# Seven block products in place of eight, for the attention groups' and the output projections of a hybrid attention/retention block

## The chip, the cores and the metric

One core of one Trainium2 chip runs the whole kernel. The metric is the device time of one execution in microseconds (us), as the median of the runs shown. All data come from and go back to the chip's own memory (HBM).

## The reference, cut to what matters

One layer on 4096 tokens of width 1024. `x` is normalised by RMS, then one input projection gives the parts of eight attention heads (width 64: q, k, v, a gate z, and a forget logit f for each head) and of four retention heads (width 128: q, k, v, gate z). The heads' outputs are gated, joined to 1024 columns, and go through an output projection, a second RMS norm and the residual sum.

```python
u    = rms_norm(h, pre_norm_gain)
proj = einsum('bsd,de->bse', u, w_in)            # 1024 -> 4104 columns
fq, fk, fv, fz, ff, rq, rk, rv, rz = split(proj)
c    = cumsum(log_sigmoid(ff + bias))
fox  = softmax(fq.fk/8 + c[t] - c[s], causal) @ fv * silu(fz)
ret  = group_norm(chunkwise_retention(rotary(rq), rotary(rk), rv)) * silu(rz)
out  = einsum('bse,ed->bsd', concat(fox, ret), w_out)
h    = h + rms_norm(out, post_norm_gain)
```

Everything is wanted in near-float32 accuracy, so each operand of a projection is held as two float16 parts, `hi` and `lo = x - hi`, and a product takes three matmul passes: hi.hi, hi.lo and lo.hi (`PASSES`).

## The kernel before, in words

**Work and groups.** Tokens are handled in 8 blocks of 512 (`NB`). The projections are cut into five groups: 0 and 1 (attention heads 0 to 3 and 4 to 7), 2 and 3 (retention heads), and 4 (output). Each input group has two parts of 512 columns: part 0 (q and k) gives its result transposed (`unit_T`: the weight is the stationary operand, 512 token columns move), part 1 (v and z) gives it token by token (`unit_N`: the tokens are stationary, 512 weight columns move; in group 0 the forget logits make it 520, run as 256 and 264). One unit is 8 steps over the 1024 inputs (`KT`) times 3 passes. A block of one part is four units, so 96 matmuls of 512 columns.

**Stages.** `phase_f0` runs group 0 over all blocks. Beside it the next block of x is loaded, normalised (`a_norm`), transposed on TensorE against the identity and split into hi and lo (`a_k`, L349 to L355), and stored to HBM as `XT`, from where the later groups load it again (`xt_load`). Then `attention` runs over 64 items (head, query block). Each of its 1152 steps makes one tile of scores (two matmuls of 512 columns into a bank), two exponentials on ScalarE (`pf`, `ph`), their difference on GpSimd (`pl`, L308), and twelve small matmuls with the values; beside that, row maxima are computed ahead (`max_tile`, L999). Between the steps, as fillers, run `fill_f1` (group 1), `fill_r` (groups 2 and 3, with the retention itself as `pump` steps) and `fill_o` (group 4). The output projection of a token block needs the last attention head on it, so nearly all of it comes after attention: the tail.

**What sets the order.** Every engine runs its instructions in the order in which the program emits them (`manual_schedule`). Fillers are given out by a credit: for each attention step of cost c, filler work of c times `ratio` is emitted, where `ratio` is what is left of `FILL_COST` over what is left of `ATT_COST`. Chains that are spawned (evictions, weight splits, norms) advance by one piece at each `tick`. All DMAs are issued from one queue, SP's (`dma`, L107), in program order: one that waits holds up those behind it. PSUM is one pool of 8 banks (`PS`). SBUF tiles come from pools by tag with fixed numbers of buffers (`BUFS`): `xh` for x, `wt` and `wn` for split weights, `rw` for raw weights, `s2` for scratch, `s4` and `xt` for 4 KB rows.

**Weights.** `w_split` scales a raw tile of 128 x 512 to `hi` on ScalarE (L217) and makes `lo` on VectorE (L147), 16 tiles for a group, each of which is usable by itself. The scale needs the largest value of the whole part first (`w_max`, L225, `w_scale`).

**The first block.** The first 256 tokens are transposed while the weights arrive; four half units (`unit_T2`) start when the scale is known and two weight tiles are split, the other weight tiles being split while they run.

**Tail.** For each of 32 row tiles n: load `MX`, find the largest value (L1177), scale (L1180), transpose (L1188), split, two units of 24 matmuls of 512 columns, then square sum (L1197), product with the gain, and the residual sum. `fetch(n + 2)` loads two tiles ahead.

Of the kernel before, what the change touches and what calls it, by code (L numbers as in the profile page):

```python
# [10 lines left out]
F16 = mybir.dt.float16  # L11
# [17 lines left out]
PASSES = ((0, 0), (0, 1), (1, 0))  # L29
COST_MM = 216.0  # L30
# [9 lines left out]
FILL_COST = 1.121e6  # L40
ATT_COST = 1.05e6
# [3 lines left out]
RMIN = 1.0  # L45
# [8 lines left out]
def kernel(  # L54
# [23 lines left out]
    KC = max(8, NB + 1)  # L78
    BUFS = dict(wt=16, wn=16, rw=2, xh=8, xt=4, kc=KC, vt=KC, s4=5, xq=4, lq=2, s2=8, z1=4, pf=2, ph=6, pl=6, sm=14, mk=2, qk=4, mr=2)
# [5 lines left out]
    SHARED = {t: "b2" for t in ('s2', 'pf', 'rw')}  # L85
# [64 lines left out]
    XT = DR("XT", [NB, KT, 128, 2, 512], F16)  # L150
# [42 lines left out]
    def w_raw(g, part, k, tag="rw"):  # L193

        rows = slice(k * 128, (k + 1) * 128)
        raw = SB(tag, [128, 512 + (FH if g == 0 and part else 0)])
        if g == 4:
            dma(raw, wo2[rows, part * 512 : (part + 1) * 512])
            return raw
        base = 0 if g < 2 else 2048 + FH  # L200
        src = w2[rows, base : base + 2048].rearrange("p (s c) -> p s c", s=4)[:, 2 * part : 2 * part + 2, (g % 2) * 256 : (g % 2) * 256 + 256]
        if g == 0 and part:
            dma(raw[:, 512:520], w2[rows, 2048 : 2048 + FH])
        dma(raw[:, 0:512].rearrange("p (s c) -> p s c", s=2), src)
        return raw
# [4 lines left out]
    def w_split(g, part, k, raw, W):  # L210

        tag = w_tag(g, part)
        n = raw.shape[1]
        wt = SB(tag, [128, 2, 512 + (FH if tag == "wn" else 0)], F16)
        hi, lo = wt[:, 0, 0:n], wt[:, 1, 0:n]
        gk = gsc[g][part][:, k : k + 1]
        nc.scalar.activation(out=hi, in_=raw, func=AF.Copy, scale=gk)  # L217
        yield 1
        stt(lo, raw, gk, hi, ALU.mult, ALU.subtract)
        for _ in range(WAGE):  # L220
            yield 1
        W.append(wt)

    def w_max(mk, i, raw):
        nc.vector.tensor_reduce(out=mk[:, i : i + 1], in_=raw, axis=AX.X, op=ALU.max, apply_absolute_value=True)  # L225
# [55 lines left out]
    def scales(g):  # L281

        sets = ((0, 1),) if g == 4 else ((0,), (1,))
        for parts in sets:
            mk = SB("mk", [128, 2 * KT])
            todo = [(part, k) for part in parts for k in range(KT)]
            raws = []
            for i in range(len(todo) + 2):
                if i < len(todo):
                    raws.append(w_raw(g, *todo[i]))  # L290
                for _ in range(SAGE):
                    yield 1
                if i >= 2:
                    w_max(mk, i - 2, raws[i - 2])
# [46 lines left out]
    def a_k(b, xs, t0, k, X):  # L341
        if t0 == 0:
            X.append(SB("kc" if b % 2 == 0 else "xh", [128, 2, 512], F16))
        o = X[k]
        n = len(xs)
        until(("a", b, t0))
        p = PS()
        for t in range(n):
            nc.tensor.transpose(p[:, t * 128 : (t + 1) * 128], xs[t][:, k * 128 : (k + 1) * 128], idf)  # L349
        sl = slice(t0 * 128, (t0 + n) * 128)  # L350
        nc.scalar.copy(out=o[:, 0, sl], in_=p[:, 0 : n * 128])
        yield 1
        tt(o[:, 1, sl], p[:, 0 : n * 128], o[:, 0, sl], ALU.subtract)
        done.add(("xh", b, t0, k))
        if t0 + n == 4:  # L355
            done.add(("x", b, k))
            for _ in range(3 if b > 1 else 20 + 3 * k if b else 12 + 2 * k):
                yield 1
            dma(XT[b, k], o)

    def xt_load(b, k):
        o = SB("xh", [128, 2, 512], F16)
        dma(o, XT[b, k])
        return o


    def unit(outs, lhs, rhss):

        for k in range(KT):
            for i, (pw, px) in enumerate(PASSES):  # L370
                for o, r in zip(outs, rhss):
# [993 lines left out]
```

## Time and profile before

| | |
|---|---|
| median of 3 runs | 3150.25 us (3149.34 to 3151.12) |
| the profiled execution: its time, its span | 3151.84 us, 3150.0 us |
| TensorE busy, weight loads | 96%, 57% |
| VectorE, ScalarE, GpSimd busy | 66%, 59%, 43% |
| mean granted TensorE clock | 0.985 of full speed |
| DMA | 284.62 MB, 90 GB/s, 31.3% of 16 engines |

The span runs from the first to the last instruction of one profiled execution; its time is 1.84 us longer. Ends of matmuls are modelled and overlap the next ones, so a matmul's mean length is not its cost: that is read from the starts of neighbouring rows in the timeline.

### The profile page before, as it was taken

Reading aid. Unit: us, or ns where it says so; the run is one execution under the profiler, and the core shown is the slowest. Engines: PE = TensorE matmul, PEld = TensorE weight load, DVE = VectorE, ACT = ScalarE, POOL = GpSimd, SP = SyncE. Lnnn points to the kernel's source line nnn. Section 1 sums busy time; section 2 is a strip of 40 time slices with the busy share of each in tenths; the row PEclk is TensorE's granted clock in tenths of the full one; section 3 lists DMA queues with packets and bytes.
Section 4 is the critical chain, followed back from the end, with each engine's and each line's share of the span. In section 5 each row is a group of like instructions: output and inputs, shape, how many; then the busy total and the mean of one; then the engine's idle time right before and its main releaser. Section 6 shows DMA issues by size and latency. Waiting matters only on the chain.

```text
span 3150.0 us, 67744 instructions
## 1 busy us (share of the span) xinstructions
PE 3029.2 (96%) x26798; PEld 1794.7 (57%) x26799; DVE 2076.8 (66%) x4372; ACT 1873.1 (59%) x3508; POOL 1351.6 (43%) x1285
## 2 busy tenths in 40 slices
PE   8999989999999999999999999999999999889999
PEld 6666555555555555665555565556556555555554
DVE  6545567446455676777678878776877786645555
ACT  4333345676677667666667675667666766653332
POOL 0000024554555455555545564556455645540000
PEclk9999999999999999999999999999999999999999
DMA  6455753223235231311114223112111321124443
GB/s 179 156 166 152 199 123 95 67 82 93 69 88 134 64 80 35 91 51 52 55 57 101 58 71 97 51 43 78 49 51 45 111 73 33 57 68 141 141 141 120
DMA packets 266174, 284.62 MB, mean 90 GB/s; under 512 B 58976, under 2 KB 212192, under 8 KB 265856
## 3 DMA queue, kind: packets, MB, share of 16 engines
q1 hardware_dynamic: 265856, 280.30, 31.3%
q8 instruction: 210, 3.44, 0.4%
q14 instruction: 108, 0.88, 0.1%
HBM read 194.88 MB, written 88.74 MB: 90 GB/s over the span
## 4 chain that ended last, share of the span: by engine, by line
PE 80%; DVE 12%; ACT 3%; issue 2%; DMA 2%; POOL 1%; SPq 1%; POOLq 0%; DVEq 0%; ACTq 0%
PE ps L104 77%; DVE mrow L999 3%; DVE s L141 2%; DVE s L144 1%; DVE sm L141 1%; DMA rw<-in_w_in_dram 1%; ACT ph L1133 1%; PE ps L1188 1%; ACT pf L1132 1%; SPq L107 1%; PE ps L349 1%; DVE sm L144 1%; DVE s L147 1%; POOL pl L308 1%; POOL sm L308 0%
## 5 line engine op out<-in xcount | busy, mean ns | idle before, releaser
L308 POOL TENSOR_TENSOR pl<-pf,ph 128x512 f16<-128x512 f32 (+3 forms) x1152 | 1281.2, 1117 | 1135.0 <-ACT ph L1133 856.8
L1132 ACT ACTIVATE pf<-ps,gsc 128x512 f32<-128x512 f32 (+3 forms) x1152 | 758.2, 658 | 694.0 <-PE ps L104 677.0
L999 DVE TENSOR_REDUCE mrow<-ps 128x1 f32<-128x512 f32 (+3 forms) x1152 | 717.6, 641 | 356.9 <-PE ps L104 345.8
L104 PE MATMUL ps<-wn,xh 128*128 128x512 f16 (+2 forms) x3840 | 852.7, 359 | 3.1 <-DVE qk L147 2.9
L1133 ACT ACTIVATE ph<-ps,gsc 128x512 f16<-128x512 f32 (+3 forms) x1152 | 754.3, 655 | 0.0
L104 PEld LDWEIGHTS <-xh 128*128 128x128 f16 x4608 | 450.2, 98 | 450.5 <-issue 22.5
L104 PE MATMUL ps<-xh,wt 128*128 128x512 f16 x2688 | 667.7, 381 | 3.4 <-DVE mrow L999 2.0
L104 PEld LDWEIGHTS <-wt 128*128 128x128 f16 x3168 | 308.9, 98 | 356.4 <-issue 24.6
L104 PEld LDWEIGHTS <-ph 128*128 128x128 f16 x8448 | 423.9, 97 | 76.0 <-issue 8.0
L104 PE MATMUL ps<-vt,ph 128*128 128x65 f16 (+1 forms) x8448 | 433.8, 195 | 10.4 <-ACT ph L1133 7.3
L104 PE MATMUL ps<-xq,kc 99*128 99x512 f16 (+3 forms) x1152 | 420.0, 365 | 14.6 <-DMA xq<-MR 9.7
L104 PE MATMUL ps<-vt,pl 128*128 128x65 f16 x4224 | 423.4, 193 | 3.8 <-POOL pl L308 3.8
L104 PE MATMUL ps<-lq,kc 128*128 128x512 f16 (+3 forms) x1152 | 419.1, 364 | 0.0
L104 PE MATMUL ps<-kc,xq 99*128 99x512 f16 (+3 forms) x1152 | 383.1, 364 | 34.3 <-DVE mrow L999 25.1
L104 PEld LDWEIGHTS <-pl 128*128 128x128 f16 x4224 | 393.3, 99 | 5.1 <-POOL pl L308 4.7
L104 PEld LDWEIGHTS <-kc 128*128 128x128 f16 (+1 forms) x3072 | 281.9, 99 | 196.8 <-issue 22.2
L141 DVE TENSOR_TENSOR s<-s,s 64x512 f32<-64x512 f32 (+1 forms) x256 | 258.6, 1010 | 33.3 <-ACT s L755 26.3
L308 POOL TENSOR_TENSOR sm<-sm,nhalf 128x4 f32<-128x4 f32 (+2 forms) x80 | 63.0, 787 | 350.5 <-DVE sm L144 308.5
L104 PEld LDWEIGHTS <-xq 99*128 99x128 f16 x1152 | 112.3, 98 | 139.4 <-issue 9.5
L104 PE MATMUL ps<-wt,xh 128*128 128x512 f16 x768 | 184.0, 381 | 0.0
L141 DVE TENSOR_TENSOR ps<-ps,maskM 128x128 f32<-128x128 f32 x256 | 75.1, 293 | 108.4 <-PE ps L104 107.6
L141 DVE TENSOR_TENSOR xh<-ps,xh 128x256 f16<-128x256 f32 (+1 forms) x128 | 70.3, 555 | 105.5 <-ACT xh L338 86.1
(120 smaller groups left out, 2525.2 us busy)
## 6 DMA issues: line engine op xcount, KB each, us to landing
xh<-XT SPq DMA_DIRECT2D x176, 256.0 KB
rw<-in_w_in_dram SPq DMA_DIRECT2D x104, 256.0 KB
xt<-in_x_dram SPq DMA_DIRECT2D x36, 512.0 KB
s<-MX SPq DMA_DIRECT2D x32, 512.0 KB
out_dram<-xt SPq DMA_DIRECT2D x31, 512.0 KB
s<-in_x_dram SPq DMA_DIRECT2D x28, 512.0 KB
VD<-s SPq DMA_DIRECT2D x16, 516.0 KB
vt<-VD SPq DMA_DIRECT2D x64, 129.0 KB
```

The costliest lines, as they stand in the source:

```text
L104: nc.tensor.matmul(out=o, lhsT=lhsT, rhs=rhs, start=start, stop=stop, skip_group_check=True)
L107: nc.sync.dma_start(out=o, in_=i)
L141: nc.vector.tensor_tensor(out=o, in0=a, in1=b, op=op)
L144: nc.vector.tensor_scalar(out=o, in0=a, scalar1=s1, scalar2=s2, op0=op0, op1=op1)
L147: nc.vector.scalar_tensor_tensor(out=o, in0=a, scalar=s, in1=b, op0=op0, op1=op1)
L308: nc.gpsimd.tensor_tensor(out=o, in0=a, in1=b, op=op)
L349: nc.tensor.transpose(p[:, t * 128 : (t + 1) * 128], xs[t][:, k * 128 : (k + 1) * 128], idf)
L999: nc.vector.tensor_reduce(out=mrow[:, t, c : c + 1], in_=p[:, 0:w], axis=AX.X, op=ALU.max)
L1132: nc.scalar.activation(out=pf[:, q0:512], in_=st[:, q0:512], func=AF.Exp, scale=es)
L1133: nc.scalar.activation(out=ph[:, q0:512], in_=st[:, q0:512], func=AF.Exp, scale=es)
L1188: nc.tensor.transpose(p[:, e * 128 : (e + 1) * 128], mxt[:, half * 4 + e, :], idf)
```

## The change

Groups 0, 1 and 4 compute each 2 x 2 block product with seven block products instead of eight, in the form with shared sums (Winograd's form of Strassen's scheme). One unit is now a whole part of a block: A is cut into 2 x 2 blocks of 256 tokens by 512 inputs, W into 512 inputs by 256 columns, and each product is 4 steps x 3 passes x 2 tiles = 24 matmuls of 256 columns (260 in group 0, part 1, where the eight forget columns are divided). Group 4 takes two row tiles at once (blocks of 128 rows by 512 inputs, and 512 by 512 weights). Groups 2 and 3 keep their units (`plain_T`, `plain_N`).

- **Sums in.** `a_k` makes four sums of the blocks of x on VectorE and splits seven operands instead of four, four of the low parts on GpSimd; they are stored as `XT` (7 x 512 KB a block), the lower left block beside them as `XA` (512 KB). `w_make` makes four sums of the weight blocks on GpSimd, and seven split tiles of 128 x 4 x 2 x 256 for a part, into pools of 7.
- **Sums out.** Products 0, 2, 4 and 5 accumulate in one bank, 1 in a second, 3 and 6 in a third (`BANK`). After 0, 2 and 4 ScalarE copies the bank to SBUF (`post`), and VectorE adds such a copy to another bank for three of the four result blocks. A bank is written on only after the copy.
- **Order.** `flow` runs a unit's products 0, then 5 and 6 of the unit before it, then 1 to 4.
- **First block.** It starts with products 0 and 1, which need only the first 256 tokens; each weight tile of a product needs half of the raw weights scaled. x of block 1 is loaded into `xt`, whose four buffers block 0 holds; from block 2 on, x is loaded at step 47 of the 56 of the block before the one that prepares it.
- **Tail.** `prep` handles a pair of row tiles in eight pieces, one after each product; the first loads `MX` for both and reads it at once. Three of four products with the gain go to GpSimd.
- **Start of group 4** waits for all weights of the group to be split, and for the last group norm.
- **Constants.** `FILL_COST` and `ATT_COST` are both 1.085e6 (1.121e6 and 1.05e6 before); K and V buffers are 8 (9 before); no pool `rw`.

```diff
+NP = 7
+BANK = (0, 1, 0, 2, 0, 0, 2)
+PLAIN = (2, 3)
-FILL_COST = 1.121e6
-ATT_COST = 1.05e6
+FILL_COST = 1.085e6
+ATT_COST = 1.085e6
-    KC = max(8, NB + 1)
-    BUFS = dict(wt=16, wn=16, rw=2, xh=8, xt=4, kc=KC, vt=KC, s4=5, ..., s2=8, z1=4, pf=2, ph=6, pl=6, sm=14, mk=2, qk=4, mr=2)
+    KC = 8
+    BUFS = dict(wt=NP, wn=NP, xh=NP, xt=4, kc=KC, vt=KC, s4=5, ..., s2=12, z1=4, pf=2, ph=6, pl=6, sm=14, mk=2, qk=2, mr=2)
...
+    def w_make(g, part, raws, W, pace=1, pool=True):
...
+        yield from scale(0)
+        yield from split(0, 0, 0)
+        yield from scale(1)
+        yield from diff((0, 0), (0, 1), (0, 0))
+        yield from split(1, 1, 0)
+        yield from split(3, 0, 0)
+        yield from diff((0, 0), (1, 1), (0, 0))
+        yield from diff((0, 1), (1, 1), (0, 1))
+        yield from split(2, 0, 0)
+        yield from diff((1, 0), (1, 0), (0, 0))
+        yield from split(4, 0, 1)
+        yield from split(5, 1, 0)
+        yield from split(6, 1, 1)
...
+    def a_k(b, xs, k, X, first=False):
...
+        nc.scalar.copy(out=e, in_=a21)
+        sp = [split(X, i, k, a, tt) for i, a in direct]
...
+        tt(c[:, 1], a11, e, ALU.subtract)
+        tt(c[:, 0], a22, e, ALU.add)
+        tt(d[:, 0], c[:, 0], a11, ALU.subtract)
+        tt(d[:, 1], a12, d[:, 0], ALU.subtract)
...
+        sp = [split(X, i, k, a, ptt) for i, a in ((2, d[:, 0]), (3, c[:, 0]), (4, c[:, 1]), (6, d[:, 1]))]
...
+        def prod(self, i):
+            b = BANK[i]
+            new = self.p[b] is None
+            while self.unread[b]:
+                tick()
+            for k in range(4):
...
+                for n, (pw, px) in enumerate(PASSES):
+                    for t in range(self.nt):
+                        mm(p[t], self.lhs(i, t, k, pw, px), self.rhs(i, t, k, pw, px), ...)
...
+        def post(self, i):
+            if i in (0, 2, 4):
+                s = self.s[i] = SB("s2", [128, self.nt, self.w])
...
+                        nc.scalar.copy(out=o, in_=p)
+                self.unread[0] -= 1
+            if i == 1:
+                self.add(0, 0, 1, self.s.pop(0))
+            elif i == 4:
+                self.add(1, 1, 2, self.s.pop(4))
+            elif i == 5:
+                yield from self.ev.run(1, 0, self.views(0))
+            elif i == 6:
+                self.add(0, 1, 2, self.s.pop(2))
...
+    def flow(units):
+        for u in units:
+            yield from u.prod(0)
+            if prev is not None:
+                yield from prev.prod(5)
+                yield from prev.prod(6)
+            for i in range(1, 5):
+                yield from u.prod(i)
+            prev = u
...
+                if n == (4 if b > 1 else 10):
+                    spawn(a_norm(xa[0:2], ("a", b, 0)))
...
+        def advance():
+            if pre[0] is None:
...
+                fetch(n + 1)
+                pre[0] = prep(n)
+            c = next(pre[0], None)
...
+        while not ready(0) or ("loaded", 4) not in done or not all(("gn", h, NB - 1) in done for h in range(RH)):
+            yield WAIT + pump(PUMP[-1])
```

## Rows read from the trace of the kernel before

**Rows 1.** The page's chain that ended last: shares by engine, by line.

```profile
PE 80%; DVE 12%; ACT 3%; issue 2%; DMA 2%; POOL 1%; SPq 1%; POOLq 0%; DVEq 0%; ACTq 0%
```

**Rows 2.** Stretches: length; busy us of PE, PEld, DVE, ACT, POOL; clock; DMA; GB/s.

```profile
0.00:80.00 80.00, 70.14 (x503) 53.01 (x505) 50.31 (x133) 35.26 (x75) 4.10 (x10) 0.91 0.69 181
126.80:173.40 46.60, 46.60 (x331) 32.41 (x329) 22.55 (x69) 17.24 (x40) 1.56 (x3) 1.00 0.46 147
240.00:400.00 160.00, 151.58 (x1051) 104.01 (x1049) 85.12 (x249) 56.62 (x127) 3.20 (x7) 0.98 0.68 183
2700.00:2830.00 130.00, 108.59 (x1066) 67.28 (x1065) 67.02 (x138) 81.99 (x148) 66.11 (x64) 0.89 0.24 73
2850.00:3050.00 200.00, 200.00 (x997) 100.17 (x996) 116.81 (x269) 66.10 (x126) 13.26 (x36) 1.00 0.45 139
```

**Rows 3.** Timeline of PE in the tail: start, length, instructions.

```profile
2952.41 5.34 PE L104 MATMUL ps<-wn,xh 128*128 128x512 f16 x24
2957.59 1.46 PE L104 MATMUL ps<-wt,xh 128*128 128x512 f16 x6
2958.88 0.60 PE L1188 MATMUL ps<-csb,s 128*128 128x128 f32 x4
2959.32 2.10 PE L104 MATMUL ps<-wt,xh 128*128 128x512 f16 x9
```

**Rows 4.** Timeline of PE in group 0 (216.01: 256 and 264 columns by turns).

```profile
173.43 14.41 PE L104 MATMUL ps<-xh,wt 128*128 128x512 f16 x66
...
216.01 4.15 PE L104 MATMUL ps<-wn,xh 128*128 128x256 f16 x36
220.00 14.41 PE L104 MATMUL ps<-kc,wt 128*128 128x512 f16 x66
```

**Rows 5.** Timeline of PE in the first block.

```profile
24.08 10.30 PE L104 MATMUL ps<-kc,wt 128*128 128x256 f16 x70 [0.43 <-DVE wt L147]
...
34.44 1.47 PE L104 MATMUL ps<-kc,wt 128*128 128x256 f16 x12
35.75 0.38 PE L349 MATMUL ps<-csb,xt 128*128 128x128 f32 x2
...
76.97 3.27 PE L104 MATMUL ps<-wn,kc 128*128 128x256 f16 x28
```

**Rows 6.** Timeline of ACT in the first block.

```profile
4.30 1.06 ACT L328 ACTIVATE s<-xt 128x1024 bf16<-128x1024 f32 x1 [2.28 <-DMA xt<-in_x_dram]
...
10.59 2.31 ACT L351 CAST kc<-ps 128x256 f16<-128x256 f32 x8 [3.66 <-PE ps L349]
22.27 1.95 ACT L217 ACTIVATE wt<-rw,gsc 128x512 f16<-128x512 f32 x3 [9.37 <-DVE gsc L144]
```

**Rows 7.** Groups by form, 80 to 240 us (DVE, ACT), whole span (POOL): busy, mean ns.

```profile
L141 DVE TENSOR_TENSOR kc<-ps,kc 128x256 f16<-128x256 f32 x32 | 13.2, 420 | 14.9 <-ACT kc L351 14.9
L351 ACT CAST kc<-ps 128x256 f16<-128x256 f32 x32 | 11.7, 370 | 25.6 <-PE ps L349 25.5
L308 POOL TENSOR_TENSOR pl<-pf,ph 128x512 f16<-128x512 f32 x960 | 1149.4, 1201 | 965.5 <-ACT ph L1133 713.8 <-PE ps L104 194.6 <-issue 28.3
L308 POOL TENSOR_TENSOR pl<-pf,ph 128x256 f16<-128x256 f32 x64 | 44.4, 694 | 70.7 <-ACT ph L1133 66.3 <-PE ps L104 3.3 <-POOL pl L308 0.7
```

**Rows 8.** Waits of PE, 480 to 1000 us, the longest: total, times, longest.

```profile
PE ps L104 <- ACT ph L1133: 1.5, 1, 1.5
```

**Rows 9.** Waits of PE, 1200 to 2600 us, the longest.

```profile
PE ps L104 <- DVE mrow L999: 29.2, 32, 4.2
```

**Rows 10.** Groups by form, 2850 to 3100 us: DVE and ACT of the tail.

```profile
L141 DVE TENSOR_TENSOR xh<-ps,xh 128x512 f16<-128x512 f32 x45 | 31.2, 692 | 58.2 <-ACT xh L338 58.2
L147 DVE SCALAR_TENSOR_TENSOR xt<-xt,sm,xt 128x1024 f32<-128x1024 f32 x22 | 28.2, 1284 | 0.8
L338 ACT CAST xh<-ps 128x512 f16<-128x512 f32 x45 | 26.4, 586 | 63.0 <-PE ps L1188 63.0
```

**Rows 11.** The page's costliest groups: a VectorE sum of the retention stage.

```profile
L141 DVE TENSOR_TENSOR s<-s,s 64x512 f32<-64x512 f32 (+1 forms) x256 | 258.6, 1010 | 33.3 <-ACT s L755 26.3
```

More of the change, by code (lines that the diff above doesn't have):

```diff
@@ L207, in w_tag @@
     def w_tag(g, part):
         return ("wt", "wn")[part if g < 4 else 1 - part]
-    def w_split(g, part, k, raw, W):
+    wfree = {"wt": NP, "wn": NP}
+    def w_make(g, part, raws, W, pace=1, pool=True):
+        w = w_cols(g, part)
         tag = w_tag(g, part)
-        n = raw.shape[1]
[L214 to L222, printed above, removed]
@@ L224, in w_max, with seg, each, split @@
-    def w_max(mk, i, raw):
-        nc.vector.tensor_reduce(out=mk[:, i : i + 1], in_=raw, axis=AX.X, op=ALU.max, apply_absolute_value=True)
+        half = len(raws) // 2
+        sub = ptt if pool else tt
+        def seg(j, c):
+            return raws[j][1][:, :, c, :]
+        def each(rows):
+            return range(rows * half, (rows + 1) * half)
+        def split(i, rows, c):
+            while not wfree[tag]:
+                yield 1
+            wfree[tag] -= 1
+            o = SB(tag, [128, 4, 2, w], F16)
+            n = 4 // half
+            for j in each(rows):
+                nc.scalar.copy(out=o[:, (j % half) * n : (j % half) * n + n, 0, :], in_=seg(j, c))
+            for _ in range(pace):
+                yield 1
+            for j in each(rows):
+                sl = slice((j % half) * n, (j % half) * n + n)
+                tt(o[:, sl, 1, :], seg(j, c), o[:, sl, 0, :], ALU.subtract)
+            W[i] = o
+            for _ in range(pace):
+                yield 1
@@ new lines, in scale, with diff @@
+        def scale(rows):
+            for j in each(rows):
+                k, r = raws[j]
+                for i in range(r.shape[1]):
+                    rr = r[:, i].rearrange("p s c -> p (s c)")
+                    nc.scalar.activation(out=rr, in_=rr, func=AF.Copy, scale=gsc[g][part][:, k + i : k + i + 1])
+                for _ in range(pace):
+                    yield 1
+        def diff(o, a, b):
+            for j in range(half):
+                sub(seg(o[0] * half + j, o[1]), seg(a[0] * half + j, a[1]), seg(b[0] * half + j, b[1]), ALU.subtract)
+            for _ in range(2 * pace):
+                yield 1
@@ L877, in fill_r @@
         W = G.W
[L878 to L880 removed]
+        for b, X, hook, last in group_blocks(G):
             vt = SB("s4", [128, 4, 256])
@@ L1252, in fill_o @@
+        for k in flow(units()):
+            yield WAIT if k is None else 3 * COST_MM
+            if k == 1:
+                c = advance()
+                if c:
+                    yield c
         flush()
```

924 lines of the change are left out of this document (591 added, 333 removed).

## The prediction

> **What bounds the kernel now.** I read the chain that ended last first: TensorE has 80% of it, and no other engine more than 12% [rows 1]. Then the busy time by stretch, to see where that share is real. In a steady block of group 0 and in the tail TensorE is busy all the time at the full clock, VectorE 48% and 58%, ScalarE 37% and 33%, GpSimd hardly at all [rows 2]. Then the timeline there, since busy matmuls may hide gaps: a block of group 0 repeats every 46.57 us (173.43 to 220.00) without a hole [rows 4]. While group 1 runs under attention, TensorE waits once, for 1.5 us [rows 8]. So in the three stages that the change touches, what a matmul saves is saved in the end, as long as the other engines keep up. The exceptions are three places that lose time: the first block (clock 0.91), the last of group 0, and the change from the last retention group to the output projection (2700 to 2830: 21 us of TensorE idle, clock 0.89) [rows 2].
>
> **What the products save.** In the tail, 24 matmuls of 512 columns take 5.18 us (2952.41 to 2957.59), 215.8 ns each [rows 3]. In the first block, 12 of 256 columns take 1.31 us (34.44 to 35.75), 109.2 ns each [rows 5]; 36 of 256 and 264 by turns take 3.99 us (216.01 to 220.00), 110.8 ns each [rows 4]. All of these load their own weights, as the new ones do, so halving the columns costs 1.2%. A unit now has 96 x 215.8 ns = 20.72 us and will have 168 x 109.2 ns = 18.35 us: 2.37 us less. There are 40 such units (8 in group 0, 16 in group 1, 16 pairs of row tiles): 94.8 us. Part 1 of group 0 goes from 192 to 168 matmuls of 260 columns, 2.66 us less, 8 times: 21.3 us. Together **116 us**. The transposes stay in number.
>
> A rule of the Trainium skill speaks against this: its page "TensorE: Matmul & The Clock Gate" (section Back-to-back issue gap) gives sustained spacings, with weight loads, of 81 ns for 128 columns and 131 ns for 512. By estimate from these, 256 columns would take some 98 ns, a unit 16.4 us after against 12.6 us before, and the change would lose. The trace has 215.8 and 109.2 ns in its place, so I give that no more than 1 in 100.
>
> **The first block.** Now real matmuls start at 24.08 and block 0 ends at 80.1 (the 28 from 76.97) [rows 5]. With an eighth of its products gone it could end 5 us sooner. But ScalarE gets most of the new work, in order. From 22.3, when the weight scale is known [rows 6], up to the point where x of block 1 is split it has: 44 pieces of weights of 512 (16 scalings, 28 copies) at some 0.63 us (3 in 1.95) = 28 us; 64 pieces of x of 256 columns at 0.29 us (8 in 2.31) = 18.5 us; six square sums at 1.05 = 6.2 us [rows 6]; seven evictions of part 0 and about half of those of part 1, some 8.5 us at 0.59 a 512 piece [rows 10]. Sum 61 us, so 83.5. The first product starts later too, since half of the weights are scaled before the first split: some 28 instead of 24. On top comes a wait: x of block 1 goes into buffers that block 0's x holds until its last transposes, and its square sum is emitted in ScalarE's queue before the last quarter of block 0's x is copied. A load takes some 3.6 us from issue to use (the first in the program is read at 4.30) [rows 6], two of them and two square sums some 6.5 us. Behind that wait stand ScalarE's copies, and behind these product 2. On SP's queue only stores wait behind the load. So block 1 starts at about 88 to 90 with 5 us of block 0 left: block 0 in effect ends at 93.5, which is 18.5 us after the 75 of a TensorE-bound start. **+19** (bounds +8, the wait hidden, to +27, where the clock falls in it too).
>
> **Group 0, steady.** A block becomes 18.35 + 18.62 us of products and 4.5 us of transposes and the rest, 41.4 us. VectorE has 22.55 us in a block [rows 2], and gets 12 more pieces of 256 columns for x, 6 for the sums out, at 0.42 [rows 7], and some small ones: 31 us, 75%. ScalarE has 17.24 and gets 20 for x and 6 copies at 0.37 [rows 7], three copies of 512: 29 us, 70%. GpSimd: 20 pieces at 0.69 and three at 1.2 [rows 7], 17 us. A copy of product 2 must be done before product 4: one product of 2.6 us covers it, and at most five casts of 0.29 stand ahead of it. DMA: 147 GB/s over 46.6 us are 6.9 MB [rows 2]; XT grows by 1.6 MB and XA adds 0.5, 9.0 MB in 41.4 us = 216 GB/s, at the same cost of a byte 0.68 of the engines, as much as 240 to 400 had with 183 GB/s [rows 2]. Block x is asked for 13 steps (9 us) before it is read. I take **+3** for stalls (0 to +25: the period stays at 46.6 if the vector engines' chain sets it).
>
> **Group 1 under attention.** The products were 1536 matmuls; the 39 us of gain are within the 116. What is added is PSUM: a unit now holds one bank through ten products, a second through five, where it held one for eight steps and an eviction, so 1.2 banks more on average and up to 4 of 8. The nearest stretch with fewer free banks is the retention stage, whose own tiles take banks: there TensorE waits 32 times for a row maximum's bank, 29.2 us in 1400 [rows 9], against none in group 1 [rows 8]. Group 1 has 0.290 of the 1.080e6 that the code counts for the fillers beside attention, so about 600 of attention's 2360 us: at that rate 12 us; **+10** (0 to +30). ScalarE's 48 copies lie beside matmuls, as it is idle for a third of that stage.
>
> **Retention and the change to group 4.** The x loads come in two pieces each, from the same prefetch distance; the weight pools allow three tiles ahead and the rest as tiles come free, 32 steps before use. I put that at 0 (0 to +6). The constants now spread the fillers evenly: by the kernel's own costs attention sums to 1.086e6 and the fillers up to group 4 to 1.08e6, so the retention ends with attention rather than 110 us before it. The idle 21 us and the slow clock there [rows 2], some 28 us, go; in their place stand, without cover, one retention's last pieces, the last group norm, the load of MX and the first `prep`: about 5 + 7 + 4 + 7 us, and 3 for the clock. **0** (-15 to +15).
>
> **Tail.** A pair of tiles goes from 22.36 to 18.35 + 16 transposes at 0.11 (four in 0.44) [rows 3] = 20.1 us. VectorE has 116.81/200 of 22.36 = 13.1 us [rows 2] and gets three splits and three sums of 512 for three gain products, at 0.69 [rows 10]: 15.1 us. In addition its first maximum now waits for MX (3.6 us as above), with all that follows on VectorE and, behind the scaling, on ScalarE: 18.7 of 20.1. The next write to bank 0 that needs ScalarE comes 9 us later, so TensorE doesn't see that wait. It does see the low part of block 0 of the next pair: made on VectorE after product 4 has begun, 1.3 us ahead of its use, and some 1.9 us of work: 0.6 us a pair. **+10** (0 to +38). The end has one sum and a gain product on GpSimd more: **+1**.
>
> The Trainium skill, "SBUF — State Buffer" (section Who interferes with whom), says that a VectorE instruction with two SBUF inputs and a GpSimd instruction that reads SBUF exclude each other. The trace agrees: such a sum takes 1010 ns beside GpSimd [rows 11], where one with a PSUM input takes 692 in the quiet tail [rows 10]. By estimate from that rule, two residual sums of 1284 ns a pair [rows 10], each held for one of seven GpSimd pieces of 1.2 us, would add 2.4 us to VectorE's 18.7 and make it the bound at 21.1 us. I count that in the second rival.
>
> **Sum.** 3150.0 - 116 + 19 + 3 + 10 + 0 + 10 + 1 = 3077 us of span, with the 1.84 us around it 3078.8. The profiled execution is 1.6 us above the median, so **3077**, own range 3050 to 3105.
>
> **Rivals.**
> *All of it hidden* (12%): only the start's lower bound and the end stay: 3150 - 116 + 8 + 1 = 3043. For it: the steady rows without holes. Against: ScalarE's 61 us in the first block.
> *The vector engines' chain sets the pace in group 0 and the tail* (18%): the loads of 75% and 93% worked out above speak for it. Then of 116 only group 1's 38 us stay in full: blocks keep 46.6 us (+33 more than my sum), pairs 21.1 to 22.4 us (+6 to +27): 3116 to 3137.
> *Slower: banks under attention* (7%). Group 1 with 4 banks leaves a step 4, for the value sums, two score tiles and a maximum. A wait costs 0.91 us (29.2/32) [rows 9]. Half of the 308 steps beside group 1 (0.290/1.086 of 1152) paying one is 140 us, in place of 10: 3207. It passes 3150 from 92 waits on. Against it: the score banks come free within the two exponentials of a step, and 32 waits in the whole retention stage.
> *Halved columns don't halve the time* (1%): from 123.3 ns a matmul of 256 columns on (20.72 us over 168) a unit gets no shorter; at the 215.8 ns of a full one, the far end, the 48 units would add some 750 us. The 109.2 and 110.8 ns above leave it no room.
>
> My forecast has 62%. The range 3040 to 3122 takes in the first rival mostly and a part of the second. A measurement of this kernel tells about 0.2%, 6 us. Faster by more: 0.88; within: 0.03; slower: 0.09.
>
> **What would show it.** In the changed profile: 24 matmuls of 256 columns in 2.62 us; a block of group 0 of 41.4 us; block 1's first product near 88 us, with ScalarE waiting for an x load near 43; waits on `mrow` or score banks in group 1, few; attention ending within some 20 us of the last retention, then TensorE idle for about 25 us; pairs of 20.7 us in the tail. I am wrong in the main if a block or a pair keeps its old length, or if TensorE's waits between 480 and 1000 us pass 30 us.

## The result and the profile after

The changed kernel takes 3254.4 us (median of 4, 3253.7 to 3262.2) against 3149.8 (4 runs beside it): a ratio of 1.034 (95% interval 1.032 to 1.036). It is 105 us slower, where 73 us less were forecast; even the rival of waits for banks under attention stood at 3207.

From the page of the kernel after, the busy time of each engine:

```profile
PE 2968.1 (91%) x29406; PEld 2065.8 (64%) x29407; DVE 2283.6 (70%) x4617; ACT 2068.5 (64%) x3984; POOL 1698.6 (52%) x1629
```

TensorE is busy for 61 us less than before (3029.2 of 3150.0), but idle for 163 us more. By stretch (span and length, then the busy time of TensorE, its weight loads, VectorE, ScalarE and GpSimd, TensorE's granted clock, DMA's share and rate): the first block, a steady block of group 0, the last block of group 0, the end of attention, the 20 us after it, a pair of the tail:

```profile
0.00:117.70 117.70, 73.54 (x474) 53.29 (x476) 77.31 (x162) 65.00 (x151) 61.12 (x69) 0.80 0.45 138
163.61:211.58 47.97, 43.99 (x379) 37.71 (x377) 32.45 (x88) 26.30 (x69) 18.64 (x26) 0.96 0.59 194
412.76:475.40 62.64, 50.78 (x417) 41.11 (x415) 41.65 (x107) 26.77 (x55) 16.31 (x12) 0.92 0.74 176
2700.00:2856.00 156.00, 128.50 (x1339) 81.26 (x1338) 105.51 (x171) 112.81 (x205) 103.81 (x87) 0.90 0.09 30
2856.00:2876.00 20.00, 5.34 (x32) 4.32 (x33) 11.06 (x29) 6.91 (x11) 2.08 (x3) 0.57 0.58 177
3049.99:3072.68 22.69, 21.31 (x195) 18.90 (x193) 15.06 (x35) 10.83 (x21) 9.70 (x11) 1.00 0.42 140
```

None of VectorE, ScalarE and GpSimd is above 68% in a steady block or a pair, so it is not the amount of their work that TensorE waits for. Block 0 ends in effect at 117.7 (80.1 before): block 1's first product starts at 112.39, with two products, 5.3 us, of block 0 still behind it. Attention, taken from the start of its first exponential to the start of its last, begins at 475.4 (424.8) and ends at 2853.7 (2813.8), and behind its end stand 398 us (336; but some 32 us of the output projection lay inside attention before).

**First block.** TensorE's timeline (start, length, engine, line, tile, count; in brackets the wait ahead of it and its releaser), and ScalarE's:

```profile
24.70 2.74 PE L110 MATMUL ps<-kc,wt 128*128 128x256 f16 x12 [5.70 <-ACT wt L252]
45.28 0.61 PE L110 MATMUL ps<-kc,wt 128*128 128x256 f16 x4 [2.42 <-ACT wt L252]
53.42 1.01 PE L110 MATMUL ps<-kc,wt 128*128 128x256 f16 x4 [2.58 <-POOL kc L396]
```
```profile
58.91 1.06 ACT L416 ACTIVATE s<-xt 128x1024 bf16<-128x1024 f32 x1 [7.80 <-DMA xt<-in_x_dram]
```

Products wait for weights, then for pieces of x, and ScalarE does stand behind the load of x(1), the x of block 1.

**A block of group 0.** ScalarE's queue ahead of the copy of product 2, then TensorE; the row of 259.50 opens the next block after that of 211.58 [rows 4 had 46.57 us]:

```profile
204.23 1.32 ACT L455 CAST xh<-s 128x256 f16<-128x256 f32 x4 [1.35 <-DVE s L147]
206.02 0.76 ACT L736 ACTIVATE s<-s 128x256 f16<-128x256 f32 x2 [0.47 <-DVE s L147]
206.68 0.63 ACT L598 COPY s<-ps 128x260 f32<-128x260 f32 x2
```
```profile
207.08 4.66 PE L110 MATMUL ps<-wn,vt 128*128 128x260 f16 x24 [2.72 <-ACT s L598]
211.58 2.78 PE L110 MATMUL ps<-xh,wt 128*128 128x256 f16 x24
214.19 2.06 PE L110 MATMUL ps<-wn,vt 128*128 128x260 f16 x17
...
255.10 4.56 PE L110 MATMUL ps<-wn,xh 128*128 128x260 f16 x24 [2.77 <-ACT s L598]
259.50 2.67 PE L110 MATMUL ps<-kc,wt 128*128 128x256 f16 x23
```

24 of 256 columns take 2.61 us (211.58 to 214.19), as forecast. But product 4 waits 2.72 us for the copy, and its own 24 then take 4.50 us (207.08 to 211.58). The copy was free to go (it waits for nothing itself) but stood in ScalarE's queue behind four casts and two scalings, and these waited for sums on VectorE.

**A pair of the tail.** VectorE, ScalarE and TensorE in turn:

```profile
3047.14 0.21 DVE L150 TENSOR_SCALAR sm<-sm,sm 128x1 f32<-128x1 f32 x1 [1.55 <-POOL sm L396]
3048.79 1.28 DVE L153 SCALAR_TENSOR_TENSOR xt<-xt,sm,xt 128x1024 f32<-128x1024 f32 x1
3049.99 0.69 DVE L147 TENSOR_TENSOR s<-ps,s 128x512 f32<-128x512 f32 x1
```
```profile
3050.77 0.63 ACT L1611 ACTIVATE s<-s 128x512 bf16<-128x512 f32 x1 [3.94 <-DVE s L147]
3051.86 0.59 ACT L598 COPY s<-ps 128x512 f32<-128x512 f32 x1
```
```profile
3052.50 0.27 PE L110 MATMUL ps<-wn,xh 128*128 128x256 f16 x1 [1.08 <-ACT s L598]
```

Read from below: product 4 waits for a copy, the copy stands behind a square, the square waits for a sum on VectorE, the sum stands behind a finished row's residual, and that waited for GpSimd.

**The entry to attention.** Attention's first 100 of 1152 steps take 243 us (223 before). TensorE loses 24.8 us there in three waits, the longest for row maxima, which go through memory:

```profile
528.91 0.59 PE L110 MATMUL ps<-xq,kc 99*128 99x512 f16 x1 [11.90 <-DMA xq<-MR]
```

**After attention** the pair's first transposes wait for the scaling of MX:

```profile
2868.55 1.76 PE L1543 MATMUL ps<-csb,s 128*128 128x128 f32 x7 [12.00 <-ACT s L1522]
```

### The profile page after: what moved, and what is told of

It is laid out like the page before. It is cut to its first block, busy times and chain, and to the rows that moved or that the text cites. A ratio compares the mean times of both kernels' runs of the same rounds, so it can differ in the third digit from the quotient of the medians.

```text
span 3251.9 us, 74066 instructions
## 1 busy us (share of the span) xinstructions
PE 2968.1 (91%) x29406; PEld 2065.8 (64%) x29407; DVE 2283.6 (70%) x4617; ACT 2068.5 (64%) x3984; POOL 1698.6 (52%) x1629
## 5 line engine op out<-in xcount | busy, mean ns | idle before, releaser
L110 PE MATMUL ps<-wn,xh 128*128 128x256 f16 (+2 forms) x4704 | 917.8, 311 | 42.8 <-ACT s L598 33.1
L110 PEld LDWEIGHTS <-xh 128*128 128x128 f16 x5856 | 577.4, 99 | 319.6 <-issue 57.4
L110 PE MATMUL ps<-xh,wt 128*128 128x256 f16 (+1 forms) x3552 | 647.2, 322 | 8.6 <-DVE mrow L1342 6.0
L110 PEld LDWEIGHTS <-wt 128*128 128x128 f16 x4224 | 417.8, 99 | 296.3 <-issue 56.6
L110 PEld LDWEIGHTS <-ph 128*128 128x128 f16 x8544 | 433.0, 97 | 58.6 <-issue 9.0
L110 PE MATMUL ps<-vt,pl 128*128 128x65 f16 x4224 | 423.9, 193 | 14.9 <-POOL pl L396 14.7
L110 PEld LDWEIGHTS <-kc 128*128 128x128 f16 (+1 forms) x2688 | 243.3, 98 | 161.3 <-DMA xq<-MR 17.8
L110 PE MATMUL ps<-wt,xh 128*128 128x256 f16 x1152 | 266.2, 279 | 0.0
L147 DVE TENSOR_TENSOR s<-ps,s 128x512 f32<-128x512 f32 (+2 forms) x280 | 149.1, 549 | 154.2 <-ACT xh L1547 45.8
L153 DVE SCALAR_TENSOR_TENSOR s<-s,s 128x256 f32<-128x256 f32 (+3 forms) x210 | 126.8, 621 | 26.8 <-ACT s L750 12.4
L396 POOL TENSOR_TENSOR xh<-s,xh 128x256 f16<-128x256 f32 (+1 forms) x112 | 99.9, 920 | 87.1 <-ACT xh L1547 64.3
```

The costliest lines, as they stand in the source:

```text
L110: nc.tensor.matmul(out=o, lhsT=lhsT, rhs=rhs, start=start, stop=stop, skip_group_check=True)
L147: nc.vector.tensor_tensor(out=o, in0=a, in1=b, op=op)
L153: nc.vector.scalar_tensor_tensor(out=o, in0=a, scalar=s, in1=b, op0=op0, op1=op1)
L396: nc.gpsimd.tensor_tensor(out=o, in0=a, in1=b, op=op)
```

## Experiments

The kernel before ran beside each group of them at 3149 to 3152 us.

### Order and timing, one edit each

**Product order** in group 0 and the tail:
```diff
-            for i in range(1, 5):
+            for i in (2, 1, 3, 4):
```


> From the third unit of group 0 on and in the tail, product 2 is taken before product 1, so its copy has two products of cover in place of one; nothing is added or taken away. Theory A (the copy of product 2 stands in ScalarE's queue behind work that waits, and one product of 2.6 us doesn't cover it): the waits of TensorE for `s` of line 598 go (2.7 us in a block of group 0, 1.1 us in a pair of the tail), and with them the slow clock of product 4 (4.5 us in place of 2.7), so a block takes about 43.5 us in place of 47.9 and a pair about 21.3 in place of 22.7: some 6 x 4.4 + 16 x 1.4 = 49 us, 3205 us in all. Rival B (ScalarE and VectorE cannot do a block's work in less than 48 us, whatever the order): the wait moves to another product, blocks and pairs keep their length, 3245 to 3255 us.

Measured: 3242.3 us. In group 0 the waits for the copies fall from 18.1 to 0.4 us and a block takes 44.6 to 44.8 (theory A):

```profile
202.88:247.68 44.80, 42.25 (x379) 36.88 (x377) 32.55 (x90) 26.62 (x71) 19.03 (x27) 1.00 0.61 202
```

The last block begins 17 us sooner, but only 12 us arrive at attention's start: its wait for keys, whose loads follow the stores of x in SP's queue, grows from 8.5 to 12.1 us, and waits for row maxima grow too. In the tail a new wait takes the place of the old one (us in all, times, longest), and pairs stay at 22.4 on average (B):

```profile
PE ps L110 <- DVE xh L147: 25.2, 13, 2.9
```

**Norm of x(1) later** (steps 16 and 20 in place of 10 and 17):

> Only the two halves of the norm of block 1 are emitted later (steps 16 and 20 in place of 10 and 17), behind the copies of the last quarter of block 0's x. Theory A (ScalarE stands still for 7.8 us behind the load of x of block 1, and the first block is paced by ScalarE): that wait goes or falls under 1 us, and block 0 ends about 8 us sooner (at 110 in place of 117.7), attention starts at 467 in place of 475. Rival B (the first block is paced by VectorE and GpSimd, which make the low parts and the differences of the weights): ScalarE's wait goes but TensorE's first block ends within 2 us of where it did.

Measured: 3251.9 us. ScalarE's wait of 7.8 us is gone, but block 1's first product stands at 112.27, where the kernel after has 112.39. Theory A falls. TensorE's wait for the normalised x(1) grew from 9.6 us:

```profile
PE ps L481 <- DVE xt L150: 15.3, 6, 8.9
```

**The planner's count** for attention back to 1.050e6:

> Only the planner's count for attention falls from 1.085e6 to 1.050e6, so the fillers are dealt out 3% faster. Theory A (the transition is dear because nothing of the output projection lies beside attention any more): the last retention ends some 60 us before attention, one to two pairs of the output projection run beside it, TensorE's 19 us with 4.6 us of work at the transition go: 3230 us, some 25 less. Rival B (the fillers of the last 150 us are held up by what they wait for, not by their budget): the retention ends where it did within 20 us, no pair runs under attention, 3250 to 3258 us.

Measured: 3252.0 us, attention's end at 2904 instead of 2854. Neither: the first pair's transposes come 70 us before attention's end, and attention grows by 51 us where the tail loses 50.

**Pieces of x closer together** in group 0:

> Only the four pieces of x of the next block in group 0 are emitted closer together (steps 24, 29, 34, 39 in place of 24, 30, 36, 42), so that the last piece's casts are in ScalarE's queue before the copy of product 2 of the part-1 unit and done sooner. Theory A (that piece's casts are what the copy stands behind): the wait of 2.7 us before product 4 of that unit shrinks to under 1 us and blocks take 44 to 45 us, some 20 us less in all. Rival B (the queue as a whole is late): the wait stays at 2 to 3 us or appears at another product, blocks stay at 47 to 48.

Measured: 3247.5 us; the block from 205.68 to 250.25 takes 44.6, its neighbours 45.0 and 45.1. Theory A for the block: the last piece's casts were what stood ahead of the copy. The time fell by 7 us and not by 20: 9 us are left at attention's start, as the wait for keys is 13.2 us here.

**The low part of combination 0 earlier** in the tail, with the new order:
```diff
             hi(0, p11)
+            lo(0, p11)
             tt(s[2], p11, s[0], ALU.subtract)
```


> The product order 0, 2, 1, 3, 4 as in the first experiment, and in the tail the low part of combination 0 is made right after its high part, ahead of two sums and one step earlier. Theory A (in the tail, once the copies are covered, one VectorE instruction emitted too late for its use holds TensorE up): the 25.2 us of waits for `xh` in the tail go, pairs shrink from 22.4 to about 20.8 us and the tail by some 22 us: 3218 us. Rival B (VectorE's chain as a whole sets the length of a pair): the wait moves on to another product, pairs stay at 22 us or more, 3235 to 3245.

Measured: 3234.9 us, pairs 22.3: rival B. The waits go from 25.2 to 4.7 us for `xh`, and come back as 15.5 us for the copies.

**Group 0's weight differences on VectorE**:

> The changed kernel with the eight differences of weights of each part of group 0 made on VectorE and not on GpSimd. Theory A (in the first block GpSimd's two-input instructions, some 2 us each, and their mutual exclusion with VectorE's pace the weights): the weights come earlier, block 0 ends 4 to 10 us sooner than 117.7, attention starts at 465 to 471 and the time is 3244 to 3250. Rival B (the chain over ScalarE's scalings, copies and VectorE's low parts paces them, with VectorE already the fuller queue): no gain or a loss of some us, attention at 473 to 480, 3252 to 3260.

Measured: 3251.0 us. Block 1 begins at 108.68, 3.7 us sooner: a little of theory A, not the cause.

### Undoing the parts

In group 0, seven products go back to eight (plain weights, four blocks of outputs by eight tiles of 128 rows), but the seven combinations of x are still made and stored:

> Group 0 goes back to eight block products (64 steps a block), but still makes and stores the seven combinations of x that group 1 reads; all else as changed. If the loss stands where the traces put it (first block, waits of group 0's blocks, not in group 1 or by the extra work on x alone): blocks take 46.5 to 47.5 us, TensorE without waits, block 0 ends near 95 in place of 117.7, and attention starts at 440 to 455 in place of 475: 3220 to 3235 us. Rival (making the combinations of x is what slows VectorE, ScalarE and GpSimd, so that TensorE waits whatever the number of products): blocks take 49 to 52 us and attention starts at 475 or later: 3250 to 3280.

Measured: 3213.9 us, blocks of 46.8, block 0 ends at 97.2, attention begins at 445: as the first theory has it, and 6 us below its range. Of the 40 us, 30 lie ahead of attention and 10 in it, and those in its first 100 of 1152 steps, which take 230 us in place of 243: how group 0 ends reaches into attention.

The output projection goes back to the code of the kernel before:

> The output projection goes back to eight block products with the kernel before's prep and its weights by tiles of 128 rows; all else as changed, the planner's counts too. If seven products lose in the tail and in the transition: a tile takes 11.2 us as before, the start of the tail loses about 9 us in place of some 30, and the end of attention gets back the waits on `pl` of GpSimd (14 us): 3215 to 3235 us. Rival (the tail's products pay for themselves and the transition's loss comes from the even spread of the fillers): 32 x 11.2 = 358 us of tiles against 363 now, with the same 20 us of idle TensorE at the transition and the same waits before it: 3245 to 3260.

Measured: 3194.9 us, 59.5 less, and below both ranges. 34 us are in the tail (364 against 398), 21 in attention (2357 against 2378), and 6 ahead of attention, where the program is the same. The 21 us come in the last 52 of attention's 1152 steps: there TensorE waits 12.9 us for GpSimd's `pl` with group 4's combinations and 2.2 without, at a granted clock of 0.86 and 0.95.

Both:

> Both of these together: seven products only in group 1, the combinations of x made in group 0 beside eight products. If the parts add: the gains of the two runs beside this add within 8 us, and group 1 keeps its 26 to 38 us: 3165 to 3205, so above or near the 3150 of before by what the start and the entry to attention still lose. Rival (group 1's gain is eaten by what its combinations cost in group 0): attention starts 25 us or more later than in the kernel before (450 or later), 3180 to 3205; else at 430 to 440 and 3125 to 3160, faster than before or the same.

Measured: 3154.4 us (ratio 1.0008, 0.9997 to 1.0019), below the range for the sum. The parts add: 40.5 + 59.5 = 100.0, measured 100.0. Steady blocks take 46.8 without waits, so making combinations beside eight products costs 0.25 us a block. What group 1 gains is lost in the first block, which ends at 97.66 (TensorE's timeline):

```profile
46.07 0.37 PE L321 MATMUL ps<-csb,sm 128*1 128x128 f32 x1 [5.40 <-DVE sm L317]
62.50 0.30 PE L483 MATMUL ps<-csb,xt 128*128 128x128 f32 x1 [4.03 <-DVE xt L150]
```

Here TensorE's own queue stands still for transposes that were issued before their input could be there. Now the norm and the pieces of x(1) and the transpose of the second weight scale come later, and the needless stores are left out (the edit is cut to this line):
```diff
+            if b + 1 < NB or i in (0, 1, 5):
                 dma(XT[b, i, :, k : k + o.shape[1]], o)
```


> Seven products in group 1 alone, as before, with two mendings. First, in block 0 the norm and the pieces of x of block 1 and the transpose of the second weight scale come later, where their inputs are there: TensorE's waits of 5.4 us (`sm`) and 8 us (`xt`) should go and block 0 end at 86 to 90 in place of 97.7 (the kernel before: 80.3). Second, the four combinations of the last block that nobody reads again are not stored, 2 MB less ahead of the loads for attention: the waits for keys (8.7 us) and row maxima (16.5 us) should shrink to about the 10 us of the kernel before. Theory A (these two places are all that group 1 alone has against it): attention starts at 420 to 428 and the time is 3125 to 3138 us. Rival B (the waits at the entry are the trip of the maxima through memory and don't hang on the stores): only the first block gains, 3140 to 3148.

Measured: **3135.8 us**, ratio 0.9952 (0.9934 to 0.9969): half a per cent faster than the kernel before. Block 0 ends at 86.0 and attention begins at 424.2, as in the kernel before: theory A by the time. At the entry to attention it is B: the waits for row maxima stay (16.5 to 14.9 us), and I had misread the wait for keys, which lies between 1700 and 2000 us and stays too. The last block of group 0 takes 52.5 us against 57.2, but the last run below has 57.9 with the same stores, so what the stores gave is open. The planner's count back in this version:

> The run before it with the planner's count for attention at the 1.050e6 of the kernel before, so that the output projection begins under attention as there. If what costs at the transition with seven products was the making of the weights of group 4 and not the planner: with eight products two to three tiles run under attention and the drop of TensorE's work at the transition (7.6 us of wait for the first scaling) is hidden, 5 to 15 us less than the run beside it. Rival (attention's end is full, as the same edit showed with seven products): the tail shortens by as much as attention grows, within 5 us of the run beside it.

Measured: 3149.6 us, 14 more: wrong on both sides. Attention grows by 43 us, the tail shrinks by 30. And the even spread in the kernel before:

> The kernel before with one number changed: its count for attention is 1.0856e6 in place of 1.050e6, so its fillers are spread evenly as in the changed kernel and the output projection begins after attention. Theory A (the even spread is worth the 14 us that it was in the run with seven products in group 1 alone): 3133 to 3140 us, and then seven products in group 1 bring nothing by themselves. Rival B (with the longer group 1 the planner hardly matters, as between the changed kernel and its own early version): 3145 to 3153 us, and the 14 us are the products'.

Measured: 3149.7 us (1.0000, 0.9991 to 1.0009): rival B. The spread alone brings nothing. But the products alone don't either: with the early count they stand at 3149.6, as the kernel before. The 14 us need both, and why is open. The stretch of attention in the kernel with the even spread and in the version of 3135.8:

```profile
423.70:2778.20 2354.50, 2264.45 (x22170) 1329.70 (x22169) 1628.72 (x3188) 1598.64 (x2931) 1311.18 (x1189) 0.99 0.25 70
```
```profile
424.20:2768.20 2344.00, 2237.32 (x23340) 1446.22 (x23339) 1685.66 (x3236) 1623.06 (x2993) 1326.71 (x1196) 0.98 0.26 76
```

TensorE is busy for 27 us less, idle for 17 more; 10.5 us are left. The first 100 of the steps lose 11 us; steps 300 to 1100, with group 1 and the retention beside them, gain 25; the last 52 lose 3. The wait for keys is 9.2 us against 4.7; that the 8 buffers for them (9 before) make it is not shown.

Group 0 by seven, mended in order, placement and stores, with the output projection by eight:

> The output projection by eight, and group 0 by seven with all that can be mended in its order: products 0, 2, 1, 3, 4, the norm and the pieces of x of block 1 a few steps later, the four unread combinations of the last block not stored. It stands beside the run with group 0 by eight (attention from 424, 3136 us). Theory A (group 0's seven products lose only by order): blocks of 44 to 45 us against 46.8, the first block ends by 105, attention starts at 425 to 440: 3136 to 3150 us. Rival B (making fourteen weight combinations and the sums out costs the first block more than seven blocks give back): attention starts at 445 to 460: 3155 to 3175 us.

Measured: 3169.1 us (1.0063, 1.0048 to 1.0078), attention from 449.9: rival B. The first steady blocks take 44.8 to 45.3 us, but block 1's first product comes at 108.8. The wait for keys at the end of group 0, 8.5 and 12.1 us above, is 1.5 here, without the unread stores.

### What holds a pair

Longer gaps between a row's steps on VectorE and GpSimd, squares later:

> The order of products and the early low part of the run before it, and in the tail alone: the squares of the two sums are emitted 4 steps later, and 4 and 5 steps are left between the links of a row's normalisation that go from VectorE to GpSimd and back, so that neither queue stands still for them. No work is added or taken away. Theory A (a pair is held at 22.3 us by the order in the queues: the copies of products 0 and 2 stand behind a square that waits for a sum that waits for GpSimd's small powers): those 2.8 us of VectorE's stalls and the 15.5 us of TensorE's waits for `s` go, pairs come to 20.7 to 21.2 us, 3210 to 3218 us. Rival B (the number of hand-overs between the engines in a pair is the limit, whatever their order): pairs stay over 22 us, 3228 to 3240.

This edit and the two after it stand on the new order with the early low part (3234.9 us). Measured: 3299.7 us, 65 more than without, which neither theory has; pairs of 27 us. Waits (in all, times, longest) show where it began:

```profile
ACT s L1522 <- DVE sm L1521: 91.1, 14, 7.5
...
PE ps L110 <- ACT s L598: 68.6, 14, 5.7
DVE sm L1519 <- DMA s<-MX: 62.9, 14, 5.3
```

A row that is stored later frees its buffer later, the next MX is loaded later, and the maximum, the scaling and the copies behind it follow. So, other buffers (for four of the seven pieces of a pair and for its second row), and MX a pair ahead:
```diff
-                    tag = "s4" if r else "xt"
+                    tag = "xh" if r else "xt"
...
                 pre[0] = prep(n)
+                fetch(n + 3)
```


> The changed kernel with the order 0, 2, 1, 3, 4 and the early low part, and in the tail four of the seven pieces and the second row's buffers lie in memory that attention and the x of group 1 have left, so that the next pair's MX can be loaded a whole pair ahead. Theory A (a pair is held by the loop load of MX, scaling, transposes, products, row, store, buffer, load): DVE's wait for MX (1.2 to 1.6 us a pair) goes, the scalings come 3 us sooner, pairs come to 20.8 to 21.3 us, 3210 to 3220 us. Rival B (the copies stand behind squares that wait for sums, and those don't hang on MX): pairs stay at 22.0 to 22.3, 3228 to 3236.

Measured: 3217.1 us, 18 less than with the old buffers, pairs of 21.08 with TensorE at the full clock: theory A.

```profile
2999.24:3020.32 21.08, 20.43 (x187) 18.07 (x186) 14.86 (x33) 10.68 (x22) 9.72 (x11) 1.00 0.46 151
```

With the gaps as well:

> The same with the longer gaps between the links of a row's normalisation and the later squares, which cost 65 us without the buffers. Theory A (those 65 us came from the buffers alone, and the gaps take VectorE's and ScalarE's stalls away): pairs of 20.5 to 21.0 us, the best of the tails, 3205 to 3215 us. Rival B (the gaps themselves put a row's work into the next pair's prep): pairs of 22 us or more, 3230 to 3290.

Measured: 3217.1 us, pairs of 21.1. The 65 us came from the old buffers and the later load that goes with them, as A has it; but the gaps bring nothing either, where A had pairs of 20.5 to 21.0.

Then the differences for group 4's weights on VectorE, in this version and in the fastest:

> The changed kernel with the mended tail (pairs of 21.1 us), and the sixteen differences of the weights of group 4 made on VectorE in place of GpSimd, where they stood in the queue with attention's `pl`. Theory A (TensorE's 13 to 14 us of waits for `pl` late in attention, and the exponentials behind them, come from these): the waits fall to about the 3 us of the runs with eight products there, attention takes 2360 to 2368 us in place of 2379, 3199 to 3208 us in all. Rival B (VectorE, at 75% there, passes the delay on to the row maxima): waits for `mrow` grow by what those for `pl` lose, 3213 to 3222 us.

Measured: 3214.1 us, attention 2376.8 against 2379.2. The waits for `pl` after 2500 fall from 14.4 to 6.1 us, and others rise (`state` 4.5 to 6.7, a retention's transposes to 6.5): rival B in its result, by other waits than it named.

> The fastest version so far (seven products in group 1 alone, 3136 us) with the output projection by seven as mended: own buffers, order, early low part, and group 4's differences on VectorE. From the parts: pairs gain 16 x 1.3 = 20 us on its 32 tiles, the tail's start loses 28, and attention loses 25 less what the run beside it gets back (0 to 15): 3153 to 3169 us. If instead the losses come from group 0's seven products reaching into attention, and vanish with them, 3115 to 3130: the best version.

Measured: 3170.3 us (1.0069, 1.0048 to 1.0091), 34 more than with the projection by eight. Attention begins 7 us later than there by the same program up to that point (57.9 us in group 0's last block), takes 2366 us against 2344, and behind it stand 372 us against 364, in spite of the shorter pairs. With eight products the first tile's transposes lie 21 us before attention's end:

```profile
2746.98 1.97 PE L1547 MATMUL ps<-csb,s 128*128 128x128 f32 x8 [7.61 <-ACT s L1539]
```

## Why the prediction was wrong

The forecast was 177 us too low. By the undone parts: output projection, -27 forecast (-38, +10, 0, +1), +59.5 measured: 86.5 (6 of them ahead of attention, where nothing differs). Group 0, -18 forecast (-40, +19, +3), +40.5 measured: 58.5. Group 1 with its combinations of x, -28 forecast (-38, +10), +4 measured, which is hardly clear of zero: 32. The sum is 177.

- **Products, -116: the pace was right** (2.61 us for 24). All that was lost was lost around them.
- **First block, "+19": measured +43** (117.7 in place of the 75 of a TensorE-bound start). I summed ScalarE's work as a queue without holes and took the wait for x(1) as the one hole. The wait was there (7.80 us) and cost nothing in the end; the queue had other holes. With plain weights the block ends at 97, with these and a better placement at 86: some 20 us come with the seven products (fourteen weight tiles, their order, the sums out: which of them is not shown), some 11 with the placement, 6 with the rest.
- **Group 0, "one product of 2.6 us covers it, and at most five casts of 0.29 stand ahead of it": the step that failed in kind.** The casts do not take 0.29 us each in the queue; they wait there for VectorE (1.35 us), and so does the copy. The product order and the closer pieces each show it, with 44.6 to 45.1 us a block. The 41.4 of the sum were not reached: a piece's transposes still wait up to 1.7 us for the low parts of the piece before.
- **Group 1, "+10 for banks": the mechanism did not come.** Between 600 and 1000 us TensorE is busy for 99.5%, so the slower rival falls too. What the forecast had no term for is the entry to attention: its first 100 steps take 20 us longer than before, 13 of them through group 0's seven products, and with the 24.8 us there TensorE's waits between 480 and 1000 us come to 29.9, just short of the 30 that were set as a sign of being wrong in the main. Of 38 us only 14 arrive in the best version.
- **Retention and the change to group 4, "0": the largest miss, with the tail.** I let the transition's idle time go because the planner spreads evenly; what made it was not the planner (both kernels are the same with either count). Seven products need a pair's two loads of MX, two scalings and all heads' norms before their first product, 15 us after attention's end, where a single tile began before it. That the last part of attention is 19 to 22 us longer with group 4 by seven is shown by undoing it in three versions; which of its instructions does it is open, as moving the differences gave 2.4 us. By estimate from these runs the start of the tail makes up some 28 us of what the output projection missed, the end of attention 21, the pairs 33.
- **Tail, "TensorE doesn't see that wait": wrong.** I had the load of MX in VectorE's chain, but counted the copies as 9 us away from it. Through five buffers a row's store releases the next load, so the chain closes on itself, and a pair takes 22.7 us: 42 us over the 20.1 of its products and transposes in sixteen pairs, where +10 stood. With other buffers a pair takes 21.08, where 20.7 were forecast: the sum of the pair was right for a kernel with buffers that were not there.
- **The rival "vector engines' chain" (18%, 3116 to 3137)** named the place rightly (blocks and pairs keep their length), but not the reason: VectorE's own work came out as reckoned (32.5 us in a block, 15.1 in a pair), and with that work the same, order brought blocks to 44.7 us and buffers pairs to 21.1. Nor did it have the price of the places between stages.

## What to carry to other kernels

A copy or cast costs its place in its engine's queue, not its duration: for each instruction that a matmul will wait for, list what stands ahead of it in that queue and what *that* waits for, engine by engine, until the list ends at something long done. When a change makes work between engines out of matmuls, it pays first where those engines have slack and the work can be far ahead (here group 1 alone, and 14 us of its 38), and last at a start, where nothing covers it. Buffers that one step frees for the next step's load belong on the path like any instruction; undoing the parts one by one and checking that they add tells more than any single wait.

## What the runs showed of the hardware

- After a wait of 2.72 us in group 0 the next 24 matmuls took 4.50 us, where 24 of this width take 2.66 at the full clock; after the one of 2.77 us they took 4.40. The granted clock behind the first stood at 0.50, the level of 1.2 GHz, so the wait cost 1.7 times its length. In the tail the clock stayed at 1.00 after 1.08 us. But the length alone does not decide: of nine waits there of 1.96 to 2.32 us, the next 24 took 4.28 us after five, and 2.62 after four, the longest (2.32 us, at 2983.76) among them. What decides is not shown. The clock behind the wait in group 0, behind that longest one and behind one of 2.17 us:

```profile
208.00:210.00 2.00, 2.00 (x11) 1.42 (x10) 0.00 (x0) 0.00 (x0) 0.00 (x0) 0.50 0.83 270
2984.00:2986.00 2.00, 2.00 (x21) 1.84 (x19) 1.74 (x3) 1.13 (x3) 0.00 (x0) 1.00 1.08 283
3030.00:3032.00 2.00, 2.00 (x13) 1.71 (x12) 1.97 (x4) 1.19 (x2) 0.00 (x0) 0.56 1.04 342
```

- Small VectorE instructions stretch beside GpSimd: in the first block two sums of 128x2 with both inputs in SBUF took 1.2 us each, against 0.16 for such sums of 128x1 in the tail, and each ended with one of GpSimd's two instructions beside it:

```profile
25.89 1.24 DVE L147 TENSOR_TENSOR sm<-sm 128x2 f32<-128x2 f32 x1
27.16 1.19 DVE L147 TENSOR_TENSOR sm<-sm,sm 128x2 f32<-128x2 f32 x1
25.45 2.88 POOL L396 TENSOR_TENSOR xh<-xh 128x512 f32<-128x512 f32 x2 [0.33 <-DMA csb<-in_cst_dram]
```

  The Trainium skill, "SBUF — State Buffer" (section Who interferes with whom), has a VectorE instruction with two SBUF inputs contend with a GpSimd instruction that reads SBUF, and the trace agrees. Taking GpSimd's differences away brought 3.7 us there.
- With the same program up to that point, attention began at 469 to 475 us in runs that left group 0 as changed, and at 424 and 431 in the two with eight products and the later norm: some us of the end of group 0 hang on something that the traces don't name.
